# One core, a two-layer decoder trunk: first weights on two queues, idle products at the start, a cast and two square sums behind a copy, logarithms two steps later

## Chip, core and metric

The kernel runs on one core of one Trainium2 chip. The metric is the device time of one execution in microseconds (us). Five engines share the work: PE multiplies matrices, ACT and DVE work element by element, POOL does small extras and issues DMAs, SP issues the weight loads.

## The reference

A decoder trunk of two layers over 256 positions of width 2048, all in float32. Layer 0 mixes with SSD heads (Mamba-2) and latent attention behind one input projection; layer 1 mixes with stick-breaking attention. Each layer ends with a SwiGLU FFN of width 5632, and each sub-layer starts with an RMSNorm.

```python
for layer in range(DEPTH):
    h = rms_norm(x, mix_norm[layer])
    if layer % 2 == 0:
        mix = ssd_mla_mixer(h, ...)      # concat(y_ssd, y_mla) @ w_out
    else:
        mix = stick_breaking_mixer(h, w_qkv, w_out)
    x = x + mix
    x = x + swiglu_ffn(rms_norm(x, ffn_norm[layer]), w_gate, w_up, w_down)
return rms_norm(x, final_norm)

# y_ssd = rms_norm(y * silu(z), ssd_norm)
# stick-breaking, per head and query block:
z = (q @ k.T) * scale
log_keep = where(mask, -softplus(z), 0)
later = cumsum(log_keep, reverse=True) - log_keep
out = where(mask, exp(log_sigmoid(z) + later), 0) @ v
```

## The kernel before

Every float32 product is done as three products of split operands. A weight tile of 512 x 512 (1 MB) is loaded by SP into a slot w, ACT casts its high part into a slot wh (L320), and DVE subtracts to leave the low part in place (L326); PE then adds hi x wh, hi x wl and lo x wh into an accumulator bank (L426, L428, L429 in project, L755 in pair). The activations are split in the same way after a transpose on PE (transpose_split: L331 for sources in fp32r words with ident_r, L333 for float32 sources with ident; then L351 on ACT, L353 on DVE). xres and xwords are two views of one buffer, the residual x in four blocks of 512 columns, one in float32, one in fp32r.

pair computes two column blocks of 512 together with seven products M1 to M7 of 4 x 4 tiles in place of eight (operand sums on one side, weight differences L702 on the other), each of twelve products on PE, and then four plain tiles c0 to c3 of 24 products each. The order of these is a list: HALF, MORE or, for the first half of each output projection, LATE = M1, M5, M3, M6, M2, M7, M4, c0, c1, c2, c3. M1, M6 and M7 share the bank z, M5 and M3 the bank p3. A sum that is needed twice is copied out of its bank by ACT (L776) before the next M adds to it; self.kept is the last such copy. The first half of the even layer's SSD output is the first place that uses LATE; there project_residual also needs scale(), the inverse root of the mean square of y, which root() computes from square sums on ACT (L316), a sum and small steps on DVE and a square root on ACT (rstd, newton, L297 to L312). root() runs as a task beside the products.

Tasks are generators; each yield n lets n ticks pass, and a tick is called by project and pair after six to eight products. PE's instructions stand in the order in which the program records them. Those of the other engines are placed by a scheduler: a smaller priority number goes first, issue_after names an instruction that has to stand ahead, and weight casts stay in their order. The first loads have priority 0, the constants 1, the weight tiles rise from 100000 (self.wprio), and URGENT is 50000.

At the start, constants() loads mix_norm and x on SP, make_identity builds ident on POOL, and a DMA on POOL copies it to ident_r. norm_block(0) transposes the first block of x in two halves of 256 columns; its rank is 99600. The blocks 1 to 3 follow between the products of the first weight tile. norm_next calls norm_block for the third and fourth block of each FFN's input with rank URGENT. In layer 1, stick_weights makes the weights of four heads: scores z, |z| and exp on ACT, the logarithm (L1102), a split of the result (parted, L320), cumulative sums on PE (L1118, L1120), a subtraction on DVE (L1121) and the last exp (L1122). There are four such groups, and stick_out uses their results (L1045) behind the third pair.

## Time and profile before

| what | value |
|---|---|
| median of 3 runs | 2378.89 us (2378.01 to 2379.22) |
| profiled execution | 2378.49 us, its span 2376.4 us |
| PE busy in the span | 2351.4 us, 11076 products |
| weight products of pair (L755), high parts | 986.0 us, x3896, 391 ns each |
| cast of a weight tile on ACT (L320) | 1874 ns mean, x399 |
| low part on DVE (L326) | 2253 ns mean, x399 |
| copy of a partial sum on ACT (L776) | 587 ns mean, x132 |
| table load on ACT | 1283 ns |

A product's length in the table is longer than the distance to the next one, since products overlap on PE. Idle time is listed in front of the group that waited, with the instruction that ended the wait behind it.

### The profile page before, as it was taken

Reading aid. Unit: us, or ns where it says so; the run is one execution under the profiler, and the core shown is the slowest. Engines: PE = TensorE matmul, PEld = TensorE weight load, DVE = VectorE, ACT = ScalarE, POOL = GpSimd, SP = SyncE. Lnnn points to the kernel's source line nnn. Section 1 sums busy time; section 2 is a strip of 40 time slices with the busy share of each in tenths; the row PEclk is TensorE's granted clock in tenths of the full one; section 3 lists DMA queues with packets and bytes.
Section 4 is the critical chain, followed back from the end, with each engine's and each line's share of the span. In section 5 each row is a group of like instructions: output and inputs, shape, how many; then the busy total and the mean of one; then the engine's idle time right before and its main releaser. Section 6 shows DMA issues by size and latency. Waiting matters only on the chain.

```text
span 2376.4 us, 28267 instructions
## 1 busy us (share of the span) xinstructions
PE 2351.4 (99%) x11076; PEld 1958.5 (82%) x11076; DVE 1987.3 (84%) x1638; ACT 1459.4 (61%) x1476; POOL 227.3 (10%) x301
## 2 busy tenths in 40 slices
PE   8999999999999999999999999999999999999998
PEld 7888878988888888888888888888888888888886
DVE  6786588578998899989887889779997988999884
ACT  6665564566755555666655686776665665556663
POOL 1342010110000000000000010000000000000011
PEclk9999999999999999999999999999999999999999
DMA  7665556545667777777776655556667777777773
GB/s 266 203 199 176 184 177 194 143 142 177 230 218 228 227 226 226 233 227 230 225 253 205 203 177 177 177 177 231 230 230 214 229 234 227 226 225 236 225 258 113
DMA packets 274901, 497.88 MB, mean 210 GB/s; under 512 B 22924, under 2 KB 48144, under 8 KB 274768
## 3 DMA queue, kind: packets, MB, share of 16 engines
q1 hardware_dynamic: 255440, 446.48, 57.4%
q0 software_dynamic: 18752, 48.55, 7.7%
q8 instruction: 87, 1.43, 0.2%
q10 hardware_dynamic: 576, 1.05, 0.1%
q14 instruction: 46, 0.38, 0.0%
HBM read 459.24 MB, written 25.20 MB: 204 GB/s over the span
## 4 chain that ended last, share of the span: by engine, by line
PE 77%; issue 5%; DVE 2%; ACT 1%; POOL 0%; POOLq 0%; ACTq 0%; DVEq 0%
PE acc L755 52%; PE acc L426 7%; PE acc L429 7%; PE acc L428 7%; PE acc L470 1%; PE tr L331 1%; DVE w L326 1%; ACT wh L320 0%; PE acc L472 0%; DVE wsum L702 0%; PE at L1477 0%; PE at L1478 0%; PE at L1045 0%; DVE wsum L326 0%; PE at L1118 0%
## 5 line engine op out<-in xcount | busy, mean ns | idle before, releaser
L326 DVE TENSOR_TENSOR w<-w,wh 128x2048 fp32r<-128x2048 f32 (+2 forms) x399 | 896.1, 2253 | 189.8 <-ACT wh L320 181.3
L755 PE MATMUL acc<-wh,s 128*128 128x512 f32 x3896 | 986.0, 391 | 6.5 <-ACT s L776 4.8
L320 ACT CAST wh<-w 128x2048 fp32r<-128x2048 f32 (+2 forms) x399 | 744.7, 1874 | 334.7 <-PE acc L429 167.3
L755 PEld LDWEIGHTS acc<-wh,s 128*128 128x128 f32 x3896 | 725.6, 188 | 156.5 <-ACT s L776 6.6
L426 PE MATMUL acc<-wh,s 128*128 128x512 f32 (+1 forms) x1216 | 483.1, 397 | 0.9 <-ACT wh L320 0.9
L429 PE MATMUL acc<-wh,s 128*128 128x512 f32 (+1 forms) x1216 | 471.5, 388 | 0.0
L428 PE MATMUL acc<-w,s 128*128 128x512 f32 (+1 forms) x1152 | 446.0, 387 | 0.2 <-DVE w L326 0.2
L755 PE MATMUL acc<-w,s 128*128 128x512 f32 x1312 | 356.4, 390 | 0.2 <-DVE w L326 0.2
L755 PEld LDWEIGHTS acc<-w,s 128*128 128x128 f32 x1312 | 246.7, 188 | 52.2 <-DVE w L326 0.6
L429 PEld LDWEIGHTS acc<-wh,s 128*128 128x128 f32 x1216 | 228.6, 188 | 47.5
L426 PEld LDWEIGHTS acc<-wh,s 128*128 128x128 f32 x1216 | 228.8, 188 | 46.0 <-issue 1.7
L428 PEld LDWEIGHTS acc<-w,s 128*128 128x128 f32 x1152 | 216.9, 188 | 42.9 <-issue 1.4
L326 DVE TENSOR_TENSOR wsum<-wsum,wh 128x2048 fp32r<-128x2048 f32 (+1 forms) x101 | 217.9, 2158 | 6.1 <-ACT wh L320 6.1
L320 ACT CAST wh<-wsum 128x2048 fp32r<-128x2048 f32 (+1 forms) x101 | 182.8, 1810 | 51.8 <-PE acc L755 29.6
L320 ACT CAST wh<-lent 128x2048 fp32r<-128x2048 f32 (+1 forms) x62 | 114.5, 1857 | 62.7 <-PE acc L429 30.3
L326 DVE TENSOR_TENSOR lent<-lent,wh 128x2048 fp32r<-128x2048 f32 (+1 forms) x62 | 137.1, 2216 | 11.1 <-ACT wh L320 10.9
L702 DVE TENSOR_TENSOR wsum<-w,wsum 128x2048 f32<-128x2048 f32 (+1 forms) x52 | 104.2, 2004 | 22.4 <-PE acc L755 18.6
L776 ACT COPY s<-acc 128x512 f32<-128x512 f32 x132 | 77.3, 587 | 69.4 <-PE acc L755 69.3
L755 PE MATMUL acc<-wsum,s 128*128 128x512 f32 x380 | 104.6, 390 | 1.0 <-DVE wsum L326 1.0
L901 POOL DMA_DIRECT2D s<-s x44 | 24.4, 556 | 808.8 <-DVE s L898 466.0
L918 POOL DMA_DIRECT2D saved<-s x64 | 56.5, 1010 | 314.9 <-ACT s L917 313.9
L755 PEld LDWEIGHTS acc<-wsum,s 128*128 128x128 f32 x380 | 71.2, 188 | 16.7 <-DVE wsum L326 1.8
(265 smaller groups left out, 1916.5 us busy)
## 6 DMA issues: line engine op xcount, KB each, us to landing
w<-in_w_down_dram SPq DMA_DIRECT2D x80, 1024.0 KB, 5.0
w<-in_w_gate_dram SPq DMA_DIRECT2D x76, 1024.0 KB, 5.1
w<-in_w_up_dram SPq DMA_DIRECT2D x76, 1024.0 KB, 5.2
w<-in_w_qkv_dram SPq DMA_DIRECT2D x48, 1024.0 KB, 5.0
w<-in_w_in_dram SPq DMA_DIRECT2D x47, 1024.0 KB, 5.1
w<-in_w_out_even_dram SPq DMA_DIRECT2D x32, 1024.0 KB, 4.9
saved<-s POOLq DMA_DIRECT2D x64, 256.0 KB, 7.3
w<-in_w_out_odd_dram SPq DMA_DIRECT2D x16, 1024.0 KB, 5.0
```

Source lines behind the costliest of these rows:

```text
L320: cast = nc.scalar.copy(hi, src).ins
L326: return nc.vector.tensor_tensor(lo, src, hi.bitcast(F32), op=ALU.subtract).ins
L331: self.nc.tensor.transpose(out.bitcast(F32R), src, self.ident_r)
L426: nc.tensor.matmul(ps[t], hi[:, ts], wh, start=k == 0, stop=False)
L428: slot.used(nc.tensor.matmul(ps[t], hi[:, ts], wl, start=False, stop=False), self.clock)
L429: nc.tensor.matmul(ps[t], lo[:, ts], wh, start=False, stop=k == nk - 1)
L470: nc.tensor.matmul(ps[:, h % 2], wh[:, hs], x, start=k == n == 0, stop=False)
L702: ins = self.nc.vector.tensor_tensor(half(o, so), half(p, sp), half(q, sq), op=ALU.subtract).ins
L755: m = nc.tensor.matmul(ps[b], x, y, start=b not in started, stop=stop, skip_group_check=True)
L776: self.kept = nc.scalar.copy(o, ps[b]).ins
L901: nc.gpsimd.dma_start(words.bitcast(F32), h[t])
L918: nc.gpsimd.dma_start(self.saved[n][:, t], s, accum_op=ALU.add)
```

## The change

Three groups of edits. At the start, mix_norm and the first quarter (256 KB) of the first weight tile are loaded through ACT's queue, the rest of that tile as one quarter and one half on SP; x's second half has priority 1 and the first weights 2. rouse makes products of a tile of ones into a scratch bank that nothing reads: five ahead of everything, one behind each half of the first block's transposes. Blocks whose norm has a rank below 100000 are transposed from xres in float32. In pair with LATE, the cast of M2's weights is placed behind the copy of M5's sum, and in root() the two square sums of y's last block behind it too and three ticks later. In stick_weights the logarithms come two ticks later and behind the last weight cast recorded so far.

```diff
@@ -208,10 +208,10 @@
         c([P, 48], "filler")
         rows_m, rows_a, rows_b = self.s2([P])[:32], self.s2([P])[:56], self.s2([P])[:120]
         with self.priority(0):
-            nc.sync.dma_start(rows_m, i["mix_norm"].rearrange("l (k p) -> (l k) p", p=P))
+            nc.scalar.dma_start(rows_m, i["mix_norm"].rearrange("l (k p) -> (l k) p", p=P))
 
         for c in (0, 256):
-            with self.priority(0):
+            with self.priority(c // 256):
                 nc.sync.dma_start(self.xres[0][:, :, c:c + 256],
                                   i["x"][0, :, c:c + 256].rearrange("(t p) d -> p t d", p=P))
         for j in range(1, 4):
@@ -249,6 +249,10 @@
     def constant_tiles(self, rows_m, rows_a, rows_b):
         nc = self.nc
         c = lambda shape, name, dt=F32: self.cp.tile(shape, dt, name=name)
+        idle = self.s2([256])
+        nc.vector.memset(idle, 1.0)
+        self.idle = idle.bitcast(BF16)
+        self.rouse(5)
         self.ident = c([P, P], "ident")
         make_identity(nc, self.ident)
         warm = self.small([P, 1], "warm")
@@ -282,6 +286,12 @@
         self.vectors(rows_m, self.vm)
         self.late_vectors = lambda: (self.vectors(rows_a, self.va), self.vectors(rows_b, self.vb))
 
+    def rouse(self, n):
+
+        out = self.tr([512])
+        for _ in range(n):
+            self.nc.tensor.matmul(out, self.idle[:, :P], self.idle, start=True, stop=True)
+
     def vectors(self, rows, v):
         m = rows.shape[0]
         pt = self.tr([m])
@@ -340,6 +350,8 @@
             for k in range(2):
                 for t in range(2):
                     self.transpose(pt[:, k, t * P:(t + 1) * P], src(t, 2 * k2 + k))
+            if rank == 99600:
+                self.rouse(1)
             hi, lo = self.s2([2, S], F32R), self.s2([2, S], F32R)
             if g is None:
                 with self.urgent() if rank == self.URGENT else self.priority(rank or self.tc.cur_priority):
@@ -388,11 +400,14 @@
         for k0 in range(0, nk, 4):
             k1 = min(nk, k0 + 4)
             res = []
+            begin = self.wprio == 100000
             with self.priority(self.wprio):
                 self.wprio += 1000
                 slot = self.wtile()
                 w, wl = slot.raw, slot.part
-                self.filled(slot, *[nc.sync.dma_start(dst, src).ins for dst, src in view(w, k0, k1)])
+                with self.priority(2 if begin else self.tc.cur_priority):
+                    self.filled(slot, *[(nc.scalar if begin and n == 0 else nc.sync).dma_start(dst, src).ins
+                                        for n, (dst, src) in enumerate(view(w, k0, k1))])
                 self.parts += 1
                 order = self.after_urgent()
                 for ins in self.first if self.wprio <= 105000 else ():
@@ -410,8 +425,7 @@
     @staticmethod
     def cols(wd, c0, n=512, r0=0, first=False):
         def view(w, k0, k1):
-            step = 2 if first and k0 == 0 else k1 - k0
-            for k in range(k0, k1, step):
+            for k, step in ((0, 1), (1, 1), (2, 2)) if first and k0 == 0 else ((k0, k1 - k0),):
                 yield (w[:, k - k0:k - k0 + step, :n],
                        wd[r0 + k * P:r0 + (k + step) * P, c0:c0 + n].rearrange("(k p) n -> p k n", p=P))
         return view
@@ -484,10 +498,11 @@
     def norm_block(self, st, j, g, wait=2, rank=None, blocks=False, spill=None, pause=2):
 
         res = []
+        x = (self.xres if rank and rank < 100000 else self.xwords)[j]
 
         def gen():
             yield from self.transpose_split(
-                lambda t, k: self.xwords[j][:, t, k * P:(k + 1) * P], res, g[:, 4 * j:4 * j + 4], wait, rank)
+                lambda t, k: x[:, t, k * P:(k + 1) * P], res, g[:, 4 * j:4 * j + 4], wait, rank)
             if j == 2:
                 st["lo"] = self.lo
             for t in range(2):
@@ -684,10 +699,10 @@
             self.filled(w, *[self.nc.sync.dma_start(dst, src).ins for dst, src in view(w.raw, k0, k0 + 4)])
         return w
 
-    def wsplit(self, w, uses, n=4, *kind):
+    def wsplit(self, w, uses, n=4, *kind, after=None):
         wh, wl = self.high()[:, :n], w.part[:, :n]
         self.parts += 1
-        with self.priority(self.wprio), self.after_urgent():
+        with self.priority(self.wprio), self.after_urgent(), self.tc.issue_after(after) if after else nullcontext():
             self.wprio += 100
             self.last_split = self.split(wh, wl, w.raw[:, :n], True)
         self.overwrite(w, self.last_split, *kind)
@@ -773,7 +788,9 @@
             if keep:
                 with self.urgent():
                     o = kept[keep] = self.s2([512])
-                    self.kept = nc.scalar.copy(o, ps[b]).ins
+                    copied = nc.scalar.copy(o, ps[b]).ins
+                    if keep == "M5":
+                        self.kept = copied
             with self.urgent():
                 for c, q, take, t in (("p2", "M1", left, 0), ("p4", "M7", left, 1), ("z", "M5", right, 1),
                                       ("p3", "M6", right, 0)):
@@ -854,7 +871,7 @@
             if m[0] == "c":
                 load(m)
                 src[m] = raw[m]
-            w = self.wsplit(src[m], 8 if m[0] == "c" else 4)
+            w = self.wsplit(src[m], 8 if m[0] == "c" else 4, after=self.kept if order is self.LATE and m == "M2" else None)
             if m[0] == "c":
                 k0 = 8 + int(m[1]) // 2 * 4
                 x = [[self.operand_tile(st, k0 + k, t) for k in range(4)] for t in range(2)]
@@ -1096,9 +1113,9 @@
             zs.append(z)
             es.append(e)
             yield 1
-        yield 2
+        yield 4
         for z, e in zip(zs, es):
-            with self.tc.issue_after(last.ins):
+            with self.tc.issue_after(last.ins), self.tc.issue_after(self.cast):
                 nc.scalar.activation(e, e, AF.Ln, bias=1.0)
             nc.vector.scalar_tensor_tensor(e, z, 0.0, e, op0=ALU.max, op1=ALU.add)
 
@@ -1178,10 +1195,11 @@
         r_u = []
 
         def root():
+            yield 7
+            for t in range(2):
+                with self.tc.issue_after(self.kept):
+                    self.square_sum(y[3][t], ssq_u[:, t, 3:4])
             yield 4
-            for t in range(2):
-                self.square_sum(y[3][t], ssq_u[:, t, 3:4])
-            yield 3
             su = self.small([P, 2], "ssqs")
             with self.priority(self.URGENT):
                 nc.vector.tensor_reduce(su, ssq_u, AX.X, ALU.add)
```

Three places in the compiled order, before and after. PE at the start: the product that turns mix_norm (L288, L298 after), the transposes of x's first block and the first weight products; after the change four more idle products (tr<-s) stand ahead of these rows. Before:

```order
L288 MATMUL tr_185<-ident,s_1_119 128x32
L331 MATMUL tr_189<-ident_r,xwords_89 128x128 x4
L331 MATMUL tr_200<-ident_r,xwords_89 128x128 x4
L426 MATMUL acc_223<-wh_65,s_15_194 128x512
L428 MATMUL acc_223<-w_69,s_15_194 128x512
L429 MATMUL acc_223<-wh_65,s_16_195 128x512
```

and after:

```order
L293 LDWEIGHTS s_8_152
L293 MATMUL tr_154<-s_8_152 128x512
L298 MATMUL tr_193<-ident,s_1_119 128x32
L343 MATMUL tr_197<-ident,xres_85 128x128 x4
L293 LDWEIGHTS s_8_152
L293 MATMUL tr_202<-s_8_152 128x512
L343 MATMUL tr_210<-ident,xres_85 128x128 x4
L293 LDWEIGHTS s_8_152
L293 MATMUL tr_215<-s_8_152 128x512
L440 MATMUL acc_235<-wh_65,s_18_204 128x512
```

An idle product stands behind each group of four transposes, and these read xres with ident.

ACT in the first output pair. The casts are of M2 (w_76), M7 (w_72), M4 (wsum_82) and c0 (w_78); the first copy (L776, L791 after) is of M5's sum, the second one, in the rows after, of M6's. Before:

```order
L320 CAST wh_65<-w_76 128x2048
L316 ACTIVATE s_293_2592,ssq_1965<-s_28_221 128x512
L316 ACTIVATE s_294_2594,ssq_1965<-s_29_222 128x512
L776 COPY s_295_2596<-acc_2557 128x512
L320 CAST wh_66<-w_72 128x2048
L320 CAST wh_67<-wsum_82 128x2048
L351 ACTIVATE s_297_2618<-tr_2613,va 128x256
L304 ACT_TABLE_LOAD
L304 ACTIVATE rsy_2646<-rsv_2645 128x2
```

and after, from the copy of M5 on:

```order
L791 COPY s_297_2605<-acc_2570 128x512
L330 CAST wh_65<-w_76 128x2048
L330 CAST wh_66<-w_72 128x2048
L330 CAST wh_67<-wsum_82 128x2048
L363 ACTIVATE s_299_2627<-tr_2622,va 128x256 x2
L363 ACTIVATE s_302_2646<-tr_2641,va 128x256 x2
L326 ACTIVATE s_304_2652,ssq_1978<-s_32_233 128x512
L326 ACTIVATE s_305_2654,ssq_1978<-s_33_234 128x512
L791 COPY s_306_2664<-acc_2569 128x512
L314 ACT_TABLE_LOAD
L314 ACTIVATE rsy_2689<-rsv_2688 128x2
L330 CAST wh_68<-w_78 128x2048
```

The squares (L316, L326 after) and M2's cast moved behind the copy, the four L351 (L363) ahead of the square root, and c0's cast now stands right behind the root.

DVE in the same pair, from the low part of M7 (w_71) over that of M4 (wsum_81) to that of c0 (w_77). Before:

```order
L326 TENSOR_TENSOR w_71<-w_72,wh_66 128x2048
L305 RECIPROCAL rsy_2646<-rsy_2646 128x2
L326 TENSOR_TENSOR wsum_81<-wsum_82,wh_67 128x2048
L309 TENSOR_TENSOR rstd_2647<-rsy_2646 128x2
L353 SCALAR_TENSOR_TENSOR s_298_2619<-tr_2613,va,s_297_2618 128x256
L310 TENSOR_TENSOR rstd_2647<-rstd_2647,rsv_2645 128x2
L353 SCALAR_TENSOR_TENSOR s_298_2619<-tr_2613,va,s_297_2618 128x256
L311 TENSOR_SCALAR rstd_2647<-rstd_2647 128x2
L353 SCALAR_TENSOR_TENSOR s_301_2638<-tr_2632,va,s_300_2637 128x256
L312 TENSOR_TENSOR rstd_2647<-rstd_2647,rsy_2646 128x2
L353 SCALAR_TENSOR_TENSOR s_301_2638<-tr_2632,va,s_300_2637 128x256
L326 TENSOR_TENSOR w_77<-w_78,wh_68 128x2048
```

and after:

```order
L336 TENSOR_TENSOR w_71<-w_72,wh_66 128x2048
L336 TENSOR_TENSOR wsum_81<-wsum_82,wh_67 128x2048
L365 SCALAR_TENSOR_TENSOR s_300_2628<-tr_2622,va,s_299_2627 128x256 x2
L365 SCALAR_TENSOR_TENSOR s_303_2647<-tr_2641,va,s_302_2646 128x256 x2
L1205 TENSOR_REDUCE ssqs_2686<-ssq_1978 128x2
L307 TENSOR_SCALAR rsv_2688<-ssqs_2686 128x2
L315 RECIPROCAL rsy_2689<-rsy_2689 128x2
L319 TENSOR_TENSOR rstd_2690<-rsy_2689 128x2
L320 TENSOR_TENSOR rstd_2690<-rstd_2690,rsv_2688 128x2
L321 TENSOR_SCALAR rstd_2690<-rstd_2690 128x2
L322 TENSOR_TENSOR rstd_2690<-rstd_2690,rsy_2689 128x2
L336 TENSOR_TENSOR w_77<-w_78,wh_68 128x2048
```

The small steps of the root stood between the low parts; now they stand together behind M4's, with the reciprocal directly ahead of c0's.

ACT at the first group's logarithms, from the second one on (L1102, L1119 after); the casts to s are splits of e, those to wh are weights. Before:

```order
L1102 ACTIVATE s_961_9732<-s_961_9732 128x384
L1102 ACTIVATE s_963_9750<-s_963_9750 128x384
L1102 ACTIVATE s_965_9767<-s_965_9767 128x384
L776 COPY s_966_9806<-acc_9634 128x512
L320 CAST s_967_9828<-s_959_9718 128x384
L320 CAST wh_68<-w_80 128x2048
L320 CAST s_969_9846<-s_961_9732 128x384
L320 CAST wh_65<-w_78 128x2048
```

and after:

```order
L1119 ACTIVATE s_965_9745<-s_965_9745 128x384
L1119 ACTIVATE s_967_9763<-s_967_9763 128x384
L1119 ACTIVATE s_969_9780<-s_969_9780 128x384
L791 COPY s_970_9811<-acc_9647 128x512
L330 CAST s_971_9855<-s_963_9731 128x384
L330 CAST wh_68<-w_80 128x2048
L330 CAST wh_65<-w_78 128x2048
L330 CAST wh_66<-w_76 128x2048
```

The logarithms stand where they stood; the second split of e has left its place behind the first weight cast.

## The prediction

> **What bounds the kernel now.** I read the page's busy line, then the waits of PE, then the timeline around each of them. The busy line says that PE works nearly the whole span:
>
> ```profile
> span 2376.4 us, 28267 instructions
> PE 2351.4 (99%) x11076; PEld 1958.5 (82%) x11076; DVE 1987.3 (84%) x1638; ACT 1459.4 (61%) x1476; POOL 227.3 (10%) x301
> ```
>
> So 2376.4 - 2351.4 = 25.0 us is all the idle time that PE has, and a change that leaves the products alone can gain only there, or where PE runs at a lower clock. Of the waits of PE (total, times, longest) two lie inside the program:
>
> ```profile
> PE acc L755 <- ACT s L776: 4.8, 3, 3.0
> ...
> PE acc L755 <- ACT wh L320: 1.6, 1, 1.6
> ```
>
> The three groups of edits lie at these two, the copy of a partial sum (L776) and a weight cast (L320) in the stick-breaking part, and at the start, where PE waits for its first data.
>
> **The partial sum.** The longest wait is in the first output pair, where M3 adds into the bank of M5 and must wait until ACT has copied M5's sum out. The timeline (start, length, engine, instruction, idle before it):
>
> ```profile
> 324.30 0.58 ACT L776 COPY s<-acc 128x512 f32<-128x512 f32 x1
> 324.37 1.07 PE L755 MATMUL acc<-wsum,s 128*128 128x512 f32 x4
> 324.77 1.90 ACT L320 CAST wh<-w 128x2048 fp32r<-128x2048 f32 x1
> 326.57 0.63 ACT L316 ACTIVATE s<-s 128x512 f32<-128x512 f32 x1
> ...
> 327.81 0.57 ACT L776 COPY s<-acc 128x512 f32<-128x512 f32 x1
> 328.43 2.77 PE L755 MATMUL acc<-wh,s 128*128 128x512 f32 x8 [2.99 <-ACT s L776]
> ...
> 329.96 2.28 DVE L326 TENSOR_TENSOR w<-w,wh 128x2048 fp32r<-128x2048 f32 x1
> ...
> 336.53 1.98 PE L755 MATMUL acc<-wh,s 128*128 128x512 f32 x8
> ...
> 344.69 0.61 PE L755 MATMUL acc<-wh,s 128*128 128x512 f32 x2
> ```
>
> M5's products end at 324.37 + 1.07 = 325.44, but ACT has a weight cast (M2's) and two square sums ahead of the copy, which starts at 327.81. The wait costs more than its 2.99 us. PE then does eight products in 2.77 us and later in 1.98, and the clock shows why (length, PE, PEld, DVE, ACT and POOL busy, granted clock, DMA share):
>
> ```profile
> 328.00:330.00 2.00, 1.57 (x6) 1.33 (x7) 2.00 (x3) 2.00 (x2) 0.00 (x0) 0.91 0.00 0
> 330.00:332.00 2.00, 2.00 (x6) 1.51 (x6) 2.00 (x2) 0.91 (x2) 0.00 (x0) 0.50 0.00 0
> 332.00:334.00 2.00, 2.00 (x10) 1.59 (x9) 2.00 (x3) 1.65 (x2) 0.00 (x0) 0.73 0.01 3
> ```
>
> The clock stands at 0.5 for 2 x (0.09 + 0.5 + 0.27) / 0.5 = 3.4 us, which loses half, 1.7 us.
>
> How the wait looks with nothing ahead of the copy stands at the same step of the odd layer:
>
> ```profile
> 1594.55 0.58 ACT L776 COPY s<-acc 128x512 f32<-128x512 f32 x1 [0.33 <-PE acc L755]
> ...
> 1595.19 1.19 PE L755 MATMUL acc<-wh,s 128*128 128x512 f32 x4 [0.68 <-ACT s L776]
> ```
>
> The change puts M2's cast and the squares behind the copy, so ACT is free at 324.88 and I expect 0.68 us here too: M3 starts at 325.44 + 0.68 = 326.12 instead of 328.43. Shorter waits (1.6 us, above) left the clock whole, so I take it to stay up. From M3 to c0 stand five parts of 2.72 us (the last three take from 336.53 to 344.69) and two groups of transposes of 0.35 (row below): 326.12 + 13.6 + 0.7 = 340.4, against 344.69. That would be 4.3 us.
>
> What is late next is c0. In the order after the change its cast stands behind the square root, the root behind the small sums on DVE, and those behind all four low parts and four L353. DVE goes from 325.5 through five operations of about 2.2 us (L702 and the low parts of M6, M2, M7 and M4; one ends each 2.2 us, as from 329.96) to 336.6; four L353 at about 0.41 (four took 1.65 us elsewhere, in a row below) give 338.2, two small ones 338.6. Then the root, about 0.2, and the cast, 1.9 as at 324.77: 340.7. PE waits 0.3 us for it. c0's low part takes another 2.28, to 343.0, where PE wants it after eight products, at 342.5: 0.5 more. Before, the root's steps lay between the low parts and c0 had slack. So 4.3 - 0.8 = 3.5 us is left. The other copies on ACT stay covered, though one barely: by the same steps M6's ends at 334.8 and M7 needs it at 335.0. The bounds: 4.3 if c0 is in time; 2.99 - 0.68 - 0.8 = 1.5 if the clock falls anyway. At the other two pairs of this order, the second of the even layer keeps its ACT order word for word, and in the odd one the copy never waited for the cast (ACT stood idle 0.33 us before it), so both count as nothing; M2's cast there is wanted two parts, 5.4 us, later.
>
> **The start.** The timeline of the first 18 us:
>
> ```profile
> 3.97 0.28 PE L288 MATMUL tr<-ident,s 32*128 32x32 f32 x1 [3.97 <-DMA s<-in_mix_norm_dram]
> ...
> 6.48 1.23 PE L331 MATMUL tr<-ident_r,xwords 128*128 128x128 f32 x8 [2.23 <-DMA xres<-in_x_dram]
> ...
> 8.64 0.80 PE L426 MATMUL acc<-wh,s 128*128 128x512 f32 x1 [0.93 <-ACT wh L320]
> ...
> 11.52 0.63 PE L429 MATMUL acc<-wh,s 128*128 128x512 f32 x1
> ...
> 11.94 0.57 PE L331 MATMUL tr<-ident_r,xwords 128*128 128x128 f32 x4
> ...
> 13.79 0.45 PE L331 MATMUL tr<-ident_r,xwords 128*128 128x128 f32 x4
> ...
> 14.08 0.47 PE L426 MATMUL acc<-wh,s 128*128 128x512 f32 x1
> ...
> 14.64 2.00 ACT L320 CAST wh<-w 128x1024 fp32r<-128x1024 f32 x2 [1.26 <-DMA w<-in_w_in_dram]
> ...
> 15.73 2.36 DVE L326 TENSOR_TENSOR w<-w,wh 128x1024 fp32r<-128x1024 f32 x2 [1.43 <-ACT wh L320]
> ...
> 16.89 0.39 PE L426 MATMUL acc<-wh,s 128*128 128x512 f32 x1
> ...
> 17.12 0.40 PE L428 MATMUL acc<-w,s 128*128 128x512 f32 x1
> ```
>
> The loads of x's other blocks, from their issue to their landing, and the window from 4 to 8 us, whose DMA share is the last figure but one:
>
> ```profile
> L219 SPq DMA_DIRECT2D xres<-in_x_dram x3: 503/862/2717, 3.3 to 6.3; - x3
> ...
> DMA to landing us min/median/max: 8.0/11.3/13.2
> ```
>
> ```profile
> 4.00:8.00 4.00, 1.48 (x9) 1.19 (x9) 0.19 (x1) 0.76 (x3) 2.71 (x6) 1.00 0.99 327
> ```
>
> The first products come 0.42 us apart (11.52 to 11.94), at 17 us 0.23 (16.89 to 17.12): PE starts at half clock. After the change the first four transposes need neither x's second half nor ident_r, mix_norm and the first 256 KB of weights come over ACT's queue, and idle products fill PE ahead of them. The transposes can start behind L288's, at 4.25 instead of 6.48, and two idle products of 0.4 us stand between them and the first product: 8.64 - 2.2 + 0.4, about 6.8, and probably at full clock. Taken at face value that is 1.8 us, and up to 1.9 more for ten products 0.19 slower than later: 3.7.
>
> The seven idle products (0.4 us each), a memset on DVE and two issues on ACT lie where these engines wait for the first data, and cost nothing; without that cover the products would cost 2.9 us. SP issues one transfer less ahead of the weights.
>
> I don't count on those 3.7 us. After six products PE turns to the transposes of x's second block, and then to the second megabyte of weights. The block is issued at 3.3 and lands 8.0 us later, at 11.3; before, PE came at 11.94. The weights land at 14.6; their cast and low part reach PE just when it wants them, 17.1. Both are transfers behind the same bytes as before, on engines that are 0.99 busy from 4 to 8 us. The new order fills only the gaps ahead of that, at most the 0.54 us by which SP issues earlier. So the block lands at 10.8 to 11.3 and PE, ready at about 8.4, waits some 2.5 us for it. The 18 products and two groups of transposes left (4.7 us at full clock) then end near 15.6, and the second product of the next weights waits for its low part until 16.5 to 16.9: a gain of 0.2 to 0.6. If the new wait pulls the clock down as the one of 2.99 us did, the 1.7 us are more than the lead of 16.89 - 15.6 = 1.3, and PE loses 0.2 to 0.4. I take 0.3 us gained, between -1 (a loss) and 1.9.
>
> The rule in the Trainium skill, "DMA: Bandwidth & Descriptors", "Issuing engines are not separate DMA queues", speaks against the two queues: transfers of all issuers run on the same 16 engines, and another issuer saves only issue time. The 0.99 agrees with it; by the rule the start would gain the 0.54 us above, without it up to 3.7.
>
> **Transposes.** The condition that picks xres instead of xwords holds for the second half of norm_next as well (rank 50000): eight groups of four transposes later in the program turn from fp32r into fp32. A group of the one kind takes 0.29 us to the next product (13.79 to 14.08), of the other 0.35:
>
> ```profile
> 307.13 0.60 PE L333 MATMUL tr<-ident,s 128*128 128x128 f32 x4
> ...
> 307.48 0.48 PE L426 MATMUL acc<-wh,s 128*128 128x512 f32 x1
> ...
> 1684.03 1.65 DVE L353 SCALAR_TENSOR_TENSOR s<-tr,va,s 128x256 fp32r<-128x256 f32 x4
> ```
>
> 8 x 0.066 = 0.5 us, on PE with nothing to hide it.
>
> **Logarithms.** Only the first of the four groups has a PE wait:
>
> ```profile
> 1370.28 1.77 ACT L1102 ACTIVATE s<-s 128x384 f32<-128x384 f32 x4
> ...
> 1372.83 1.90 ACT L320 CAST wh<-w 128x2048 fp32r<-128x2048 f32 x1
> ...
> 1374.78 2.11 PE L755 MATMUL acc<-wh,s 128*128 128x512 f32 x8 [1.58 <-ACT wh L320]
> ```
>
> ```profile
> 1584.70 0.53 ACT L1122 ACTIVATE spare<-spare 128x384 f32<-128x384 f32 x1 [2.54 <-DVE spare L1121]
> ...
> 1600.77 0.59 PE L1045 MATMUL at<-spare,s 128*128 128x256 f32 x2
> ```
>
> In the compiled order the logarithms still stand ahead of that cast; what moves is the second split of e and all behind it, one place back, and the cumulative sums on PE twelve products later. The exponentials that follow have slack: the last one of the last group starts at 1584.70, PE wants the first tile of its kind at 1600.77 and takes it in order, so a delay of two steps, 2.7 us, is covered. So nothing is gained: 0, between 1.6 gained (the wait gone) and 0.9 lost (a cast late as at 8.64).
>
> **Sum.** 3.5 + 0.3 - 0.5 + 0 = 3.3 us off. The profiled execution took 2378.49, its span and 2.1 us around it; that gives 2375.2. The median of the runs is 0.4 higher, 2378.89, and 3.3 below it is 2375.6; I say 2375.5. No change can be told from noise within about 0.2%, 4.76 us, so the likeliest outcome counts as the same.
>
> **Rivals.** (1) The start pays: x's second block and the second weights land with the first ones, 1.5 to 2 us earlier, and 1.5 to 3.7 us are gained; 3.5 + 2.6 - 0.5 gives 2373.3, with the logarithms' wait gone too 2371.7. For it speaks that PE waited 2.23 us for x at a time when 256 KB of it could have been enough; against it the DMA share of 0.99. Chance 0.2. (2) Half of the gain on the partial sum is lost: the clock falls all the same, or c0 waits longer; 1.5 + 0.3 - 0.5 gives 2377.6. Chance 0.2. (3) Slower: c0's cast behind the root. If the DVE chain is 2 us later than worked out, the wait grows to 2.8 us, the size at which the clock fell before, and 1.7 us go with it: 4.3 - 2.8 - 1.7 + 0.3 - 0.5 = -0.4, 2379.3. It decides from a wait of some 2.2 us; against it, four of the five operations only follow one another. Chance 0.07; over 4.76 us slower, three such waits, 0.03. (4) The idle products and the wait for x's block leave PE at half clock some 3.4 us longer: a start 2 us worse than counted, 2377.6. For it speaks the fall behind 2.99 us, against it the shorter waits that passed. Chance 0.1. The Trainium skill, "TensorE: Matmul & The Clock Gate", Part 1, would have it so only behind an idle window of about 3.4 us; the trace shows a fall behind 2.99 us.
>
> That leaves 0.4 for the forecast, by itself 2374.3 to 2376.5. The range to 8 in 10 leaves out the ends of (1) and (3): 2372.6 to 2378.4. Faster by over 0.2% means below 2374.1: rival (1) and the lower edge of the forecast, 0.22. Slower 0.03, the same 0.75.
>
> **What would show it.** In the profile after: the wait of L755 on the copy near 324 us at 0.7 instead of 2.99, and a clock of 1.00 behind it; a new wait of PE on c0's cast or low part some 15 us later; a wait of 2 to 3 us of the second block's transposes on x near 8 us; 1.58 us still there in the stick part; the 40 transposes of this line that turn into fp32 at 0.35 us a group. I am wrong if the second weights land before 13 us, if c0 is in time, or if the cast at 1374 no longer makes PE wait.

## The result, and the profile after

The changed kernel takes 2374.34 us (median of 21 runs, 2373.92 to 2375.41) against 2378.53 us (21 runs, 2376.31 to 2381.70) of the kernel before on the same chip: ratio 0.9983, 95% interval 0.9976 to 0.9989. 4.2 us are gained, clear of the spread, but a little less than the 0.2% that count as a difference here. One later execution of the changed kernel, in the group of changed_again below, took 4160.03 us at a mean granted clock of 0.674 and is left out of its median. The profiled execution took 2374.24 us. Its busy line, and PE's waits of the kernel's own instructions (total, times, longest):

```profile
span 2372.2 us, 28286 instructions
PE 2354.9 (99%) x11083; PEld 1959.4 (83%) x11083; DVE 1987.8 (84%) x1639; ACT 1458.9 (62%) x1476; POOL 227.2 (10%) x301
```

```profile
PE acc L770 <- ACT s L791: 2.6, 3, 1.2
...
PE acc L770 <- ACT wh L330: 1.6, 1, 1.6
...
PE tr L343 <- DMA xres<-in_x_dram: 0.6, 1, 0.6
PE acc L770 <- DVE w L336: 0.4, 2, 0.2
```

The wait on the copy (L791, formerly L776) has lost its 3.0; the one on the weight cast (L330, formerly L320) is as it was. The timeline of the first output pair (start, length, engine, instruction, idle before it):

```profile
324.26 0.58 ACT L791 COPY s<-acc 128x512 f32<-128x512 f32 x1 [0.61 <-PE acc L770]
...
324.74 3.72 ACT L330 CAST wh<-w 128x2048 fp32r<-128x2048 f32 x2
...
324.90 2.11 PE L770 MATMUL acc<-wh,s 128*128 128x512 f32 x8 [0.68 <-ACT s L791]
...
337.34 3.70 ACT L330 CAST wh<-w 128x2048 fp32r<-128x2048 f32 x2
...
339.27 6.69 DVE L336 TENSOR_TENSOR w<-w,wh 128x2048 fp32r<-128x2048 f32 x3 [0.84 <-ACT wh L330]
...
339.59 1.98 PE L770 MATMUL acc<-wh,s 128*128 128x512 f32 x8
...
341.61 0.77 PEld L770 LDWEIGHTS acc<-w,s 128*128 128x128 f32 x4 [0.47 <-DVE w L336]
```

The copy now stands ahead of the cast, M3 waits 0.68 us, and c0's cast is done at 339.24, in time for PE at 339.59; only its low part makes PE wait. The clock behind M3 (length, PE, PEld, DVE, ACT, POOL busy, granted clock, DMA share, GB/s):

```profile
328.00:330.00 2.00, 2.00 (x14) 1.71 (x13) 2.00 (x2) 2.00 (x2) 0.00 (x0) 1.00 0.38 54
```

1.00 instead of 0.91 and then 0.50. The start:

```profile
7.42 0.99 PE L440 MATMUL acc<-wh,s 128*128 128x512 f32 x1
8.20 0.63 PE L442 MATMUL acc<-w,s 128*128 128x512 f32 x1
...
10.34 0.68 PE L341 MATMUL tr<-ident_r,xwords 128*128 128x128 f32 x4
...
13.42 1.05 ACT L330 CAST wh<-w 128x1024 fp32r<-128x1024 f32 x1 [1.48 <-DMA w<-in_w_in_dram]
...
15.71 0.40 PE L440 MATMUL acc<-wh,s 128*128 128x512 f32 x1
15.95 0.40 PE L442 MATMUL acc<-w,s 128*128 128x512 f32 x1
```

The second weights arrive at 13.4, not 14.6, and their low part is used at 15.95, not 17.12.

How far the changed kernel is ahead, by the start of the same product in both traces:

| place | before | after | ahead |
|---|---|---|---|
| second weights' first low-part product | 17.12 | 15.95 | 1.17 |
| M3 of the first output pair | 328.43 | 324.90 | 3.53 |
| c0, first product | 344.69 | 339.59 | 5.10 |
| part behind the first FFN's transposes | 632.16 | 627.48 | 4.68 |
| a product behind the fourth group's logarithms | 1534.02 | 1529.77 | 4.25 |
| end of the span | 2376.4 | 2372.2 | 4.2 |

So the start brought 1.2, M3's wait and its clock 3.9, and 0.9 were given back: 0.35 at c0's low part, 0.5 around 1517 us, and some 0.1 elsewhere. The start differs between executions of one kernel: in a second profile of the changed kernel (changed_again, below) the first row of this table would have 0.57 in place of 1.17.

### The profile page after: what moved, and what is told of

It is laid out like the page before. It is cut to its first block, busy times and chain, and to the rows that moved or that the text cites. A ratio compares the mean times of both kernels' runs of the same rounds, so it can differ in the third digit from the quotient of the medians.

```text
span 2372.2 us, 28286 instructions
## 1 busy us (share of the span) xinstructions
PE 2354.9 (99%) x11083; PEld 1959.4 (83%) x11083; DVE 1987.8 (84%) x1639; ACT 1458.9 (62%) x1476; POOL 227.2 (10%) x301
## 4 chain that ended last, share of the span: by engine, by line
PE 89%; issue 6%; DVE 2%; ACT 2%; POOL 0%; DMA 0%; SPq 0%; POOLq 0%; ACTq 0%; DVEq 0%
PE acc L770 51%; PE acc L440 11%; PE acc L443 11%; PE acc L442 10%; PE acc L484 1%; DVE w L336 1%; ACT wh L330 1%; PE tr L341 1%; PE at L1423 1%; PE acc L486 0%; DVE wsum L717 0%; PE tr L343 0%; DVE wsum L336 0%; PE at L1495 0%; PE at L1496 0%
## 5 line engine op out<-in xcount | busy, mean ns | idle before, releaser
L330 ACT CAST wh<-w 128x2048 fp32r<-128x2048 f32 (+2 forms) x399 | 744.2, 1874 | 331.0 <-PE acc L443 154.1
L330 ACT CAST wh<-wsum 128x2048 fp32r<-128x2048 f32 (+1 forms) x101 | 182.7, 1809 | 50.2 <-PE acc L770 26.6
L330 ACT CAST wh<-lent 128x2048 fp32r<-128x2048 f32 (+1 forms) x62 | 114.5, 1857 | 61.7 <-PE acc L443 24.0
L791 ACT COPY s<-acc 128x512 f32<-128x512 f32 x132 | 77.3, 587 | 70.6 <-PE acc L770 70.6
```

What stands on the lines that cost most here:

```text
L330: cast = nc.scalar.copy(hi, src).ins
L791: copied = nc.scalar.copy(o, ps[b]).ins
```

## Experiments

Each kernel ran 11 times, beside the kernel before on the same chip; ratios are to it. The list is spread over three chips: on that of cast_alone, norm_on_sp and fp32r_all the kernel before took 2379.54 us (27 runs), on that of x_on_act 2379.32 (15), on that of all the others 2377.97 (33) or 2378.10 (34). Medians of two kernels from different chips are therefore compared with their traces beside them. In the profiles the mean granted clock is 0.999 where the clock never fell between the start and the end, and 0.998 where it fell once (before, start_alone, spread_logs), so it also tells of the runs without a profile.

**Each half by itself.** start_alone is the kernel before with the edits at the start (fp32 for the first block alone); sum_alone has the partial-sum edits alone:

```diff
+ after=self.kept if order is self.LATE and m == "M2"      # M2's cast
+ yield 7; square_sum(...) behind self.kept; yield 4       # root()
```

> The kernel before with the edits at the start alone (two queues, idle products, first block in fp32). Theory A, that the start gains by earlier landings: the second weight tile's first product comes near 15.7 us instead of 16.89, all of it 1.2 us earlier, and the wait of M3 stays at 2.99 us; 1.2 us faster than before. Rival, that two issuers save issue time only: 0.3 to 0.5 us faster, product near 16.4. Theory C, that the gain at the start is given back at the next waits: no difference.

> The kernel before with M2's cast and the two squares behind the copy of M5, nothing else. Theory A: the wait of M3 falls from 2.99 to 0.68 (2.3 us), the clock stays at 1.00 (1.6 us), c0 waits 0.35 us for its low part: 3.6 us faster than before. Rival, that c0 waits 0.8 us as predicted: 3.1 us. Rival, that the clock falls at another place of this pair instead: 2.0 us.

start_alone: 2377.16 us (2375.66 to 2378.28), ratio 0.9995 (0.9986 to 1.0004). sum_alone: 2375.12 us (2374.36 to 2376.66), ratio 0.9987 (0.9978 to 0.9996). By medians that is 0.8 and 2.85 us. In sum_alone's trace M3's lead grows by 2.3 at its start and 1.6 more up to the next part, and 0.35 are lost at c0's low part, as theory A had it: 3.6 us. The median gives less, and the interval holds both. The mean clock of the runs accounts for the difference: of the 33 runs of the kernel before, 15 show 0.999 and a median of 2377.14, and all of sum_alone's show 0.999. These two are 2.0 us apart, about the 2.3 less 0.35 that remain without the half clock; against the 11 runs with 0.998 (2378.33) it is 3.2. So the 1.6 us of half clock seem to be paid in some executions of the kernel before and not in others. For start_alone, runs of equal clock are 1.0 us (0.999) and 1.2 us (0.998) faster than before. Its traces agree: the product that the kernel before starts at 36.19 us starts at 36.10 to 36.99 in the four profiles with the old start and at 34.98 to 35.74 in the five with the new one (after, changed_again, start_alone, keep_two, spread_logs).

In start_alone the old wait stands, and the clock falls behind it:

```profile
13.83 1.05 ACT L330 CAST wh<-w 128x1024 fp32r<-128x1024 f32 x1 [2.26 <-DMA w<-in_w_in_dram]
...
16.20 0.50 PE L442 MATMUL acc<-w,s 128*128 128x512 f32 x1 [0.70 <-DVE w L336]
...
327.46 1.93 PE L770 MATMUL acc<-wh,s 128*128 128x512 f32 x4 [2.99 <-ACT s L791]
```

```profile
328.00:330.00 2.00, 2.00 (x6) 1.57 (x5) 2.00 (x3) 1.22 (x1) 0.00 (x0) 0.50 0.00 0
```

Here PE runs ahead and waits 0.70 us for the second weights' low part: that weight tile bounds the start. In the profile of the changed kernel, where the clock rose only at 11.49 us, PE came later and did not wait for it (15.95).

**Half of the move.** On the kernel before, squares_alone moves the two squares and leaves M2's cast ahead of the copy; cast_alone moves the cast and leaves the squares.

> The kernel before with only the two squares moved; M2's cast stays ahead of the copy of M5. The copy starts near 326.8, M3 waits 1.9 to 2.0 us instead of 2.99. Theory A, that the clock falls only behind a wait that takes more than about 60% of a 3.4 us window: clock 1.00 behind it, 1.0 + 1.6 - 0.35 = 2.3 us faster than before. Rival, that half a window is enough: clock 0.5 behind it, 0.7 us faster.

> The kernel before with only M2's cast behind the copy of M5; the two squares stay ahead of it and the root stays between the low parts. The squares take 1.24 us from 324.9, the copy starts near 326.1, M3 waits 1.3 us instead of 2.99. Theory A, that the clock falls only where a wait fills more than about 55 to 60% of a 3.4 us window: clock 1.00 behind it, and c0 in time since its cast is not behind a late root: 1.7 + 1.6 = 3.3 us less than the kernel before where that one's clock falls, 2375.2 by the median. Rival, that each part of the move brings its own time: 1.7 us.

squares_alone: 2375.60 us (2375.13 to 2378.18), ratio 0.9990 (0.9981 to 0.9998). cast_alone: 2375.40 us (2374.51 to 2376.54), ratio 0.9983 (0.9974 to 0.9992). M3's start in either, and the clock behind the longer of the two waits:

```profile
327.09 2.11 PE L755 MATMUL acc<-wh,s 128*128 128x512 f32 x8 [1.77 <-ACT s L776]
```

```profile
326.00:328.00 2.00, 0.91 (x4) 0.78 (x5) 2.00 (x2) 2.00 (x3) 0.00 (x0) 1.00 0.51 197
328.00:330.00 2.00, 2.00 (x11) 1.59 (x10) 2.00 (x2) 1.57 (x2) 0.00 (x0) 1.00 0.00 0
```

```profile
327.29 2.11 PE L755 MATMUL acc<-wh,s 128*128 128x512 f32 x8 [1.19 <-ACT s L776]
```

With 1.77 us of wait the clock stays at 1.00, as theory A had it in both: the first 1.2 us taken off the wait also save the 1.6 us at half clock, and the rest of the move adds only its own length. In squares_alone nothing is lost at c0, so that it gains 2.8 us by its trace (2.4 by medians), not 2.3. Its rival, half a window, is not refuted: the clock's records lie on steps of 3.41 us from its rise, and of the 1.77 us at most 49% of one step were idle. cast_alone has no wait at c0, since its root stays between the low parts; that costs it 0.5 us at M3 (1.19 against 0.68), so it gains 3.4 us by its trace, 0.2 less than sum_alone.

**The start, part by part.** changed_again is the changed kernel; no_idle leaves out rouse; one_queue puts mix_norm and the first weights back on SP (two words nc.scalar to nc.sync).

> The changed kernel as it is, to stand beside the others of this group: 2374.3 us, its runs within 1 us of each other, while those of the kernel before spread over 4 to 5 us. In its profile the clock may rise at another moment than 11.49 us; theory A, that the second weights bound the start, expects their first low-part product at 15.9 to 16.3 all the same.

> The changed kernel without the seven idle products. Theory A, that the earlier landings make the gain at the start and the idle products only protect it from a late rise of the clock: the second weights land at 13.4 to 13.9 as with them; where the clock rises before 12 us the time is the same, where it rises at 12 to 14 us up to 0.8 us are lost; median 0.2 to 0.5 us slower than the changed kernel, runs spread over 2 us. Rival, that the idle products make the gain at the start: 1.0 to 1.2 us slower. Rival, that they do nothing: the same.

> The changed kernel with mix_norm and the first 256 KB of weights back on SP's queue, the idle products and the rest kept. Theory A, that the second queue brings the second weights forward by 1.0 us: they land near 14.6 instead of 13.4 to 13.8, and the start is 0.8 to 1.0 us later. Rival, issue time only: two issues of about 0.55 us less on SP, they land 0.5 us later than in the changed kernel and 0.3 to 0.5 us are lost. Rival, that the order of the bytes counts and not the queue: no difference.

changed_again 2374.6 us (2373.96 to 2375.70), ratio 0.9982 (0.9973 to 0.9991); no_idle 2374.56 (2373.84 to 2375.22), ratio 0.9984 (0.9975 to 0.9992); one_queue 2376.40 (2375.06 to 2377.72), ratio 0.9992 (0.9983 to 1.0001). The idle products bring nothing, neither in the median nor in the spread (my theory A had expected 0.2 to 0.5 and 2 us of spread). They do go with an earlier clock: its first record at 1.00 stands at 13.18 us in no_idle's trace, at 12.22 to 14.00 in the four with the old start, and at 6.22 to 11.49 in the five with the new one. The second queue brings 1.8 us, more than both theories had. Part of that seems to be the clock: seven of one_queue's runs show 0.998, none of the changed kernel's; its other four have a median of 2375.99, 1.4 behind. one_queue's profile:

```profile
11.30 0.50 PE L341 MATMUL tr<-ident_r,xwords 128*128 128x128 f32 x4 [2.02 <-DMA hp<-in_a_log_dram]
...
15.11 1.05 ACT L330 CAST wh<-w 128x1024 fp32r<-128x1024 f32 x1 [2.42 <-DMA w<-in_w_in_dram]
...
17.48 0.50 PE L442 MATMUL acc<-w,s 128*128 128x512 f32 x1 [0.77 <-DVE w L336]
```

SP issues the second weights 0.94 us later than in the changed kernel (4.24 against 3.30), they land 0.9 to 1.7 us later, and the wait of 2 us that I had predicted for the changed kernel stands here. (The releaser named is a small transfer; x's second block landed at 11.2.)

norm_on_sp and fp32r_all take the best version (keep_two, below) apart: mix_norm back on SP, or the first block's transposes back in fp32r words with ident_r.

> keep_two with mix_norm back on SP's queue, the first 256 KB of weights still on ACT's. SP issues everything behind it 0.5 us later (one_queue: 0.94 for two issues). Theory A, that each issue less on SP brings the later loads forward by its own time: x's second block lands near 10.8, the second weights near 14.2, 0.5 us slower than keep_two, and in runs where the clock is up early more. Rival, that only the first weights' own queue counts: no difference, 2373.7.

> keep_two with the first block's transposes back in fp32r words too, so that they wait for the copy of ident by POOL's DMA, which landed 5.5 to 6.2 us from the start in earlier runs. Theory A, that the second weights bound the start: the first transposes start near 5.6 to 6.2 instead of 4.3, the first product comes 0.2 us later at most, since x's second half lands at 5.8 to 6.3 anyway; no difference, 2373.7. Rival, that the fp32 first block makes part of the gain: 0.5 us slower.

norm_on_sp: 2374.06 us (2373.39 to 2374.58), ratio 0.9978 (0.9969 to 0.9987). fp32r_all: 2376.05 us (2375.12 to 2377.41), ratio 0.9987 (0.9978 to 0.9996). By medians they are 0.3 and 2.3 us behind keep_two, which ran on another chip, and 2.0 us apart from each other on one chip. The traces put the difference at the start: the product that keep_two starts at 35.24 us starts at 35.65 in norm_on_sp and at 38.85 in fp32r_all, and from there to the end of the span all three take 2336.5 to 2336.6. So mix_norm on SP costs 0.4 us, about one issue of 0.5; fp32r words cost some 2 us by the medians and 3.6 in the profiled execution, the slowest of its eleven, where I had expected nothing. Its PE:

```profile
4.05 0.31 PE L298 MATMUL tr<-ident,s 32*128 32x32 f32 x1
7.76 0.75 PE L341 MATMUL tr<-ident_r,xwords 128*128 128x128 f32 x4 [3.40 <-DMA ident_r<-ident]
...
9.95 0.80 PE L440 MATMUL acc<-wh,s 128*128 128x512 f32 x1
10.95 0.79 PE L442 MATMUL acc<-w,s 128*128 128x512 f32 x1 [0.21 <-DVE w L336]
...
15.12 0.63 PE L440 MATMUL acc<-wh,s 128*128 128x512 f32 x1
15.55 0.63 PE L442 MATMUL acc<-w,s 128*128 128x512 f32 x1
```

and the landing of that copy (issue line, KB, us from issue to landing), before and in fp32r_all:

```profile
ident_r<-ident POOLq DMA_DIRECT2D x1, 64.0 KB, 3.8
```

```profile
ident_r<-ident POOLq DMA_DIRECT2D x1, 64.0 KB, 5.9
```

The small copy takes 2 us longer, and the first product comes at 9.95 instead of 7.66 in keep_two. In the traces with both loads on ACT's queue the copy takes 5.0 to 6.4 us, in norm_on_sp 4.1, in one_queue 3.3, with the old start 3.8 to 4.4. So it is slower where both loads moved; that the weights in flight delay it is my reading. The first product explains 2.3 of the 3.6 us. The rest goes with the clock: the products still come 0.43 us apart at 15.5, since the clock rises at 16.72 and not at 6.22 as in keep_two; whether the wait of 3.40 delays that rise, no run took apart. This start is later than any of the old one (38.85 against 36.10 to 36.99), so reading xres with ident is what lets the second queue pay.

x_on_act is keep_two with x's second half issued by ACT as well.

> keep_two with the second half of x's first block (256 KB) issued by ACT too, ahead of the first weights there. SP issues everything behind it 0.5 us earlier. Theory A, that each issue less on SP brings the second block of x and the second weights forward by its own time and that these bound the start: second block of x near 9.6 to 9.9, second weights near 13.1, the low part of theirs 0.3 to 0.5 us earlier, 2373.3 to 2373.5. Rival, that the first product is the bound now: x's second half is issued no earlier than before (behind mix_norm on ACT) and the first weights on ACT 0.5 us later, so the first product comes 0.2 to 0.5 us later than 7.3 to 7.9, and nothing is gained or 0.2 us are lost.

2376.73 us (2374.71 to 2377.05), ratio 0.9988 (0.9979 to 0.9997), 3 us behind keep_two by medians of two chips; in the profiled execution (2375.65) the product of 35.24 us starts at 37.19, 1.95 later, and the rest takes 2336.5 to 2336.6 here too. That is the rival, and worse than it said.

```profile
8.62 0.62 ACT L330 CAST wh<-w 128x512 fp32r<-128x512 f32 x1 [2.34 <-DMA w<-in_w_in_dram]
...
9.29 0.79 PE L440 MATMUL acc<-wh,s 128*128 128x512 f32 x1 [1.42 <-ACT wh L330]
```

```profile
w<-in_w_in_dram ACTq DMA_DIRECT2D x1, 256.0 KB, 6.8
```

The first weights, issued on ACT 0.5 us later (1.80 against 1.29), landed 1.6 us later than in keep_two (8.6 against 7.0); PE waited 1.42 us for their cast, and the clock rose at 14.02. That SP's weights and x's second block, issued 0.5 us earlier, were by then ahead of them is my reading; no run took it apart.

**Logarithms and transposes.** keep_two is the changed kernel with the logarithms as before and fp32 for the first block alone:

```diff
-        x = (self.xres if rank and rank < 100000 else self.xwords)[j]
+        x = (self.xres if rank == 99600 else self.xwords)[j]
```

> The changed kernel with the logarithms as before, and fp32 transposes for the first block alone (the eight groups of the FFN's input back in fp32r). Theory A, from the trace: the logarithms cost 0.46 us in the last of the four groups (a new wait of 0.2 at 1517.4 and one of 0.3 just ahead), the fp32 groups next to nothing, since a wait behind them takes most of it back: 0.5 to 0.6 us faster than the changed kernel, 2373.8. Rival, as predicted: the fp32 groups cost 0.5 and the logarithms 0, which would also give 2373.8, but with the new wait at 1517.4 still there and the step at 617 to 626 us 0.4 us shorter without the wait of 0.3 coming back at 632. Rival: neither matters, 2374.3.

2373.74 us (2373.32 to 2374.58), ratio 0.9981 (0.9972 to 0.9990), 0.6 to 0.8 us faster than the changed kernel. The changed kernel at the fourth group's logarithms:

```profile
1515.07 1.69 PEld L770 LDWEIGHTS acc<-wh,s 128*128 128x128 f32 x8 [0.32 <-ACT wh L330]
...
1517.40 1.19 PE L770 MATMUL acc<-w,s 128*128 128x512 f32 x4 [0.21 <-DVE w L336]
```

keep_two has neither wait; from 1387 to 1534 us it gains 0.5 us on the changed kernel. The part behind the first FFN's transposes, before and in keep_two:

```profile
632.16 1.20 PE L755 MATMUL acc<-wsum,s 128*128 128x512 f32 x4 [0.35 <-DVE wsum L326]
```

```profile
627.50 1.21 PE L770 MATMUL acc<-wsum,s 128*128 128x512 f32 x4 [0.36 <-DVE wsum L336]
```

In the changed kernel this part starts at 627.48 without a wait: the four fp32 groups ahead of it take 0.09 us more each, and the wait shrinks by the same. So theory A, with its three signs.

spread_logs is keep_two with the first group's four logarithms two steps apart, each behind the last cast recorded.

> keep_two with the first group's four logarithms apart from each other, two steps between them and behind the last cast recorded each time, so that a weight cast stands between them on ACT. Theory A, that the 1.59 us of wait near 1370 us are the table load and the four logarithms in a row ahead of the cast: the wait goes, 0.3 to 0.6 us come back in the next three parts, 1.0 to 1.4 us faster than keep_two, about 2372.6. Rival, that the wait moves to the next cast whole: no gain, 2373.7. Rival, that the later sums of this group make PE wait behind the third pair: slower than keep_two.

2376.67 us (2375.95 to 2377.64), ratio 0.9992 (0.9983 to 1.0000): 2.9 us slower than keep_two. The wait of 1.59 at 1370 us is gone, and PE gains 1.4 us on keep_two there, so the logarithms ahead of that cast were its cause; but the cumulative sums that follow moved, and a transpose waits for their scratch bank:

```profile
1399.25 0.66 PE L379 MATMUL tr<-ident,s 128*128 128x128 f32 x4 [2.16 <-DVE spare L1142]
```

```profile
1400.00:1402.00 2.00, 2.00 (x7) 1.59 (x6) 2.00 (x2) 2.00 (x4) 0.00 (x0) 0.60 0.00 0
```

A wait of 2.16 us, and the clock falls behind it: the third rival, with the price of the partial sum.

## Why the prediction was right, and where it was not

The forecast (2375.5, range 2372.6 to 2378.4, within 0.2% of before) held; its terms held less well. By the traces 4.2 us came where 3.3 were summed. That it came so near is in part luck: the start gave 0.9 more than counted and the transposes cost 0.4 less, while the logarithms cost 0.5 that were not counted.

- **Partial sum, 3.5 predicted, 3.5 to 3.6 found in the traces, 2.85 by sum_alone's median.** The wait of 0.68, the 2.3 us less at M3 and the clock of 1.00 came as worked out; the half clock was worth 1.6, not 1.7. The prediction took it as paid in every execution; by the mean clocks above it seems to be paid in 18 of those 33 of the kernel before. c0's loss was 0.35, not 0.8: DVE's chain was ready 0.2 us earlier than worked out, and PE came 0.4 us later (14.7 us from M3 to c0, not 14.3). That c0's cast would be late was wrong; that its low part would be was right.
- **Start, 0.3 predicted, 1.2 in the profile, 0.8 by start_alone's median (whose interval takes in none).** The step that failed is the wait of 2.5 us for x's second block. It rested on a first product at 6.8, probably at full clock, on a block that lands at 10.8 to 11.3 and on weights that land at most 0.54 us earlier. The first product came at 7.3 to 7.9 in the profiles of the changed start with its full set of edits, since x's second half landed at 5.8 to 6.8 and the first weights shortly behind; in two of these five profiles, that of the result among them, PE ran at half clock until 11 us (products 0.43 apart), and the block landed at 10.0 to 10.7. PE then waited 0 to 0.7 us for the block. The second weights landed at 13.4 to 14.2, mostly below the 14.1 to 14.6 that I had allowed (14.2 to 14.7 in the four profiles with the old start). The line of 4 to 8 us with a clock of 1.00 says nothing against half clock: ahead of a trace's first clock record that column reads 1.00, and there the distance of the products tells the clock. Rival (1) was too large, rival (4) did not occur.
- **What I overlooked there.** I held the idle products for a part of the gain and the fp32 first block for a detail. The idle products are worth nothing (no_idle); the fp32 first block is worth some 2 us or more beside the second queue (fp32r_all), because PE no longer waits for the copy of ident_r, which is slower there.
- **Transposes, 0.5 lost predicted, about 0.1 found.** "Nothing to hide it" was wrong. PE's list of waits had the cover, a low part of a weight sum with two waits of up to 0.6 us, and I had not looked at where it stood.
- **Logarithms, 0 predicted, 0.5 lost.** The first group was as I read it. I had looked at that one alone, since only it made PE wait before; in the fourth the later logarithms put a cast and its low part behind time.

How the kernel before spreads over 5 us and the changed one over 1.5 goes with the granted clock: of the 33 runs of before beside the first four experiments, those with a mean clock of 0.999 took 2377.1 us (median of 15), with 0.998 2378.3 (11), with 0.997 2380.0 (7). All 21 runs of the changed kernel show 0.999.

## What to carry to other kernels

Price a wait of PE with what the clock loses behind it, and shorten such waits first to a length behind which it stayed up (1.8 us here): half of an edit can bring most of its gain. Before moving a load to another queue, list what else is in flight and which small copy the next engine waits for; the same 0.5 us of issue time was worth 0.4 us at one transfer (norm_on_sp) and minus 1.9 us or more at another (x_on_act). An edit that shifts work by a few steps at one place shifts it at every place that shares the code: read each of them, also those that do not wait yet, and look in the list of waits for the cover that an added cost may fall into.

## What the runs showed of the hardware

- The clock fell to 0.50 behind PE waits of 2.99 us (before, start_alone) and 2.16 us (spread_logs), and stayed at 1.00 behind 2.02 us (one_queue), 1.77, 1.59, 1.19 and 0.68 us. Length alone does not decide. The clock's records lie on steps of 3.41 us counted from its rise; at each fall inside the program PE had been idle for 63 to 88% of the step that ended there (63% in spread_logs, 64% in before, 88% in start_alone), and in none of these traces' other steps for more than 49%, since the 2.02 us lie across two. That a wait of 2.99 us can also lie across two steps would explain the 15 of 33 runs with 0.999; those runs have no trace that shows it. The Trainium skill, "TensorE: Matmul & The Clock Gate", Part 1, has the clock fall behind an idle window of some 3.4 us; here 2.16 us within one step were enough. It also says that the window runs freely, so that the rise differs from run to run; that agrees: the clock rose at 6.22 to 11.49 us in the five profiles with the new start, so that two early products were 0.43 us apart in the changed kernel's profile (8.63 to 9.06) and the same products 0.24 in keep_two's (8.72 to 8.96).
- Issue order set the landings at the start: 0.94 us later on SP meant 0.9 to 1.7 us later on arrival. The Trainium skill, "DMA: Bandwidth & Descriptors", "Issuing engines are not separate DMA queues", says that another issuer only saves issue time. For the second weights that is about what was found; for the first weights in x_on_act, 0.5 us of issue cost 1.6 us at landing, so there the saving of issue time was not the whole effect.
- A copy of 64 KB on POOL's queue took 3.8 us to land before, 3.3 in one_queue, and 5.9 us in fp32r_all, where the weights were issued earlier.
